# Fixing the order of matrix products, loads and gathers in the expert part of a layer

## The chip, the cores and the metric

The kernel runs on one core of one Trainium2 chip. The metric is the device time of one launch in microseconds (us). Before the change the median of three runs is 2456.3 us (2455.87 to 2461.42). The core has five engines that take instructions in order from queues of their own: TensorE (PE) for matrix products, VectorE (DVE), ScalarE (ACT), GpSimd (POOL) and SyncE (SP). SP, ACT and POOL also issue DMA transfers. An instruction that waits for something holds up all that stands behind it on its engine.

## The reference, cut to what matters

The layer mixes 256 tokens of width 2048 by an mLSTM and by differential attention, and then passes each token through experts that it picks itself (PEER). Only this last part is touched by the change:

```
q = h @ w_pq                                    # 8 heads, two halves each
s = einsum(q, sub_keys)                         # 128 scores per half
s1, i1 = top_k(s[half 0], 16);  s2, i2 = top_k(s[half 1], 16)
top_s, pos = top_k(s1[:, None] + s2[None, :], 16)     # 16 of 256 pairs
idx = (i1 * 128 + i2) at pos                    # 16 experts of 16384 per head
g   = softmax(top_s)
act = gelu(h . expert_u[idx])                   # expert_u: 16384 x 2048
out = sum over the picked experts of g * act * expert_v[idx]
```

A token has 8 x 16 = 128 picked experts. An expert has a first index i1 and a second i2, each of 128 values.

## The kernel before, in words

Everything up to the queries runs until 1167 us of the profiled execution and is untouched, instruction by instruction. Two stages follow.

**The stage of the up-projections, 1167 to 2059 us.** The kernel doesn't gather rows of `expert_u`; it reads all of it, 128 MB, as 256 loads of 512 KB on SP's queue (line 94), two for each value of i1. A load lands in a `raw` tile, ACT copies it to a rounded `hi` (line 108), DVE, and for every fourth POOL, makes the remainder `lo` (line 111), and PE multiplies all 256 tokens with `hi` and `lo` in pairs of products (lines 1191 and 1192): 16 pairs for each i1. The result goes through GELU and is written to a table in memory, `ag_dram`, that has a row for each (i1, i2).

Beside this loop runs a second program, a Python generator (`plan`, line 1376) of which `pump(rate)` does so many steps after each half of an i1. It has the picks of the tokens (`retrieve`, twice, for 128 tokens each), the gate map (`gate_map`, twice) and the lists (`lists`). The gate map turns picks into a dense table: for four tokens at a time `one_hots` (line 1202) makes two one-hot tiles, `o1` by ACT (five activations) and `o2` by POOL (four comparisons, line 1209), PE multiplies them (line 1243), ACT copies the product to `gates`, and SP writes `gates` beside the activations into `ag_dram` in 32 pieces of 512 KB (line 1221), on the same queue as the loads of `expert_u`. The lists sort the experts that are used at all into 99 blocks of 128, by which groups of 32 tokens use them; their one-hots come from the same helper, with PE's products in line 1355. A count, `n_over`, tells whether any expert found no place.

**The stage of the down-projections, 2059 to about 2435 us.** The blocks are multiplied with rows of `expert_v`. A row block (1 MB, 128 rows of 8 KB) is gathered by POOL into one of eight `vraw` halves (line 1409, source `expert_v`), and its gates and activations by another gather from `ag_dram` into an `ag` tile (same line, 128x512 for a block that serves both token halves, 128x256 else). DVE multiplies gate and activation (`w`, line 1446, or line 1443 for the small ones), ACT and DVE split the product into two parts (`l`, lines 1430 and 1431), ACT and DVE split the rows as before, and PE adds up 24 products (a block for both token halves, called B here), 12 (a block for one half, S) or 16 slower ones for a group of four blocks that serve 32 tokens each (G, line 1511, its rows not split). The list ITEMS has 65 entries; from the seventh on it runs G B S B B G B S B B ..., and from the 36th G B B S B G .... A `vraw` half is free again when PE has used both halves of its tile; eight halves hold about one round from G to G.

**What sets the order.** The program is recorded in the order in which Python runs it, and a scheduler then moves instructions within each engine by its own estimate of times. An instruction that is given to `tc.keep_in_program_order` keeps its place among the others so marked on its engine. `next_item(n)` (line 1456) records what the item n of the list needs: first the row gathers of later items, as far as buffers are free, then the gate gathers up to item n + 1; before the change the scheduler moved both as it saw fit.

Of the kernel before, what the change touches and what calls it, by code (L numbers as in the profile page):

```python
# [19 lines left out]
F32 = mybir.dt.float32  # L20
# [10 lines left out]
P = 128  # L31
# [42 lines left out]
def build(tc, a, dump=None):  # L74
    nc = tc.nc
    mm = nc.tensor.matmul
    dump = dump or {}

# [7 lines left out]
    def col(shape, name, src=None, dt=F32):  # L86
# [3 lines left out]
        return t  # L90

    def load(src, pool, bufs, queue=nc.sync):
# [8 lines left out]
    def stage(src, ring=None):  # L101
# [10 lines left out]
        return h, l  # L112

    by_four = [False]

# [996 lines left out]
    def retrieve(t):  # L1112
        def scores(t, i):
            ps = psG.tile([P, 4, P], F32, name="g", tag="g")
            for ii in range(4):
                mm(ps[:, ii, :], lhsT=qT[:, i + ii, t * P:(t + 1) * P], rhs=skT[:, i + ii, :], start=True, stop=True)
# [41 lines left out]
        for s in range(2):  # L1158
            oh = tk.tile([P, HEADS, 16, 16], F32, name="oh", tag="oh", bufs=1)
            for h in range(HEADS):  # L1160
                nc.vector.tensor_tensor(oh[:, h], b3(posf[:, s, h, :], 16),
                                        iota[:, 0:16].unsqueeze(1).to_broadcast([P, 16, 16]), op=OP.is_equal)
                nc.gpsimd.tensor_tensor(oh[:, h], oh[:, h], ti4[:, h, s, :].unsqueeze(1).to_broadcast([P, 16, 16]),
                                        op=OP.mult)
                if h % 2:
                    yield
            r = tk.tile([P, HEADS, 16], F32, name="ix", tag=f"ix{s}", bufs=1)
            nc.vector.reduce_sum(r, oh, axis=AX.X)
            ii.append(r)
            yield  # L1170
        ps = psG.tile([P, 4, P], F32, name="g", tag="g")
        for i, src in enumerate((ii[0], ii[1], e)):
            nc.tensor.transpose(ps[:, i, :], src.rearrange("p h i -> p (h i)"), ident)
            nc.vector.tensor_copy(slots[i][:, t * P:(t + 1) * P], ps[:, i, :])
# [6 lines left out]
    def u_pair(i1, rate):  # L1181
        pss = []
        for e in range(2):
            ps = psS.tile([P, 2, T], F32, name="s", tag="s")
            flat = ps.rearrange("p s t -> p (s t)")
            for hf_ in range(2):
                hl = take()
                for kk in range(8):
                    k = hf_ * 8 + kk
                    w = slice(kk * P, (kk + 1) * P)  # L1190
                    mm(flat, lhsT=hl[0][:, w], rhs=h2hl[k], start=k == 0, stop=False, skip_group_check=True)  # L1191
                    mm(ps[:, 1], lhsT=hl[1][:, w], rhs=h2[0][k], start=False, stop=k == 15, skip_group_check=True)  # L1192
                pump(rate)
            pss.append(ps)
        return pss
# [6 lines left out]
    def one_hots(rows, cols, factor, n=4, width=P):  # L1202
        o1 = gm.tile([P, 4, P], F32, name="o1", tag="o1", bufs=2)
        for i in range(n):
            nc.scalar.activation(o1[:, i], iota, AF.Abs, bias=rows[:, i:i + 1], scale=-1.0)
        nc.scalar.activation(o1[:, 0:n], o1[:, 0:n], AF.Relu, bias=ones[:, 0:1], scale=-1.0)
        o2 = gm.tile([P, 4, P], F32, name="o2", tag="o2", bufs=2)
# [19 lines left out]
    def gate_map(t):  # L1227
# [3 lines left out]

        nxt = hots(0)
        yield
        for hf_ in range(2):
            gates = [gm.tile([P, P // 2, HT], F32, name="gates", tag="gates", bufs=4) for _ in range(2)]
            for q in range(0, HT, 4):
                o1, o2 = nxt
                at = hf_ * HT + q + 4
                if at < P:
                    nxt = hots(at)  # L1240
                ps = psG.tile([P, 4, P], F32, name="g", tag="g")
                for i in range(4):
                    mm(ps[:, i, :], lhsT=o1[:, i], rhs=o2[:, i], start=True, stop=True)  # L1243
                for j in range(2):
# [14 lines left out]
    def lists():  # L1259
# [34 lines left out]
        def fill(kind, first):  # L1294
# [3 lines left out]
                        for _ in range(2))  # L1298
            mm(pre, lhsT=tri, rhs=flat, start=True, stop=True)
            mm(tot, lhsT=ones, rhs=flat, start=True, stop=True)  # L1300
            nc.vector.memset(put[:, 0:n], 0.0)
# [44 lines left out]

        nxt = hots(0)
        ps = psG.tile([P, 4, P], F32, name="g", tag="g")
        yield
        for i in range(0, N_LIST, 4):  # L1350
            o1, o2 = nxt
            if i + 4 < N_LIST:
                nxt = hots(i + 4)
            for j in range(min(4, N_LIST - i)):
                mm(ps[:, 0, 0:N_BLOCKS], lhsT=o1[:, j], rhs=o2[:, j, 0:N_BLOCKS], start=i + j == 0,  # L1355
                   stop=i + j == N_LIST - 1)
            yield
        mm(ps[:, 1, 0:N_LIST], lhsT=ones, rhs=over, start=True, stop=True)
        nc.vector.reduce_sum(t0[:, 0:1], ps[:, 1, 0:N_LIST], axis=AX.X)
# [168 lines left out]

    rest = nc.values_load(n_over[0:1, 0:1], min_val=0, max_val=N_EXPERTS)
    with tc.If(rest > 0):  # L1530
# [32 lines left out]
    def residual(t, c):  # L1563
        w = slice(c * 512, (c + 1) * 512)
        x = x1[t][:, w]
        y = fn.tile([P, 512], F32, name="yf", tag="yf", bufs=2)
        nc.vector.tensor_tensor(y, out_acc[t][c], g2[:, w], op=OP.mult)
# [107 lines left out]
```

## Time and profile before

| | us |
|---|---|
| median of three runs | 2456.3 |
| the profiled execution | 2458.69 |
| its span on the core | 2456.8 |
| PE busy in it | 2335.6 (95%) |
| stage of the up-projections | 1167 to 2059 |
| stage of the down-projections, with the tail | 2059 to 2456.8 |

The span runs from the first to the last instruction of the core; 1.9 us of the execution lie outside it. Busy times of engines overlap; what a stage costs is read from the engine that works without gaps in it, and from what this engine waited for where it did not. PE's busy time includes products that run at half the clock, so the granted clock of a stretch belongs to it.

### The profile page before, as it was taken

Reading aid. Unit: us, or ns where it says so; the run is one execution under the profiler, and the core shown is the slowest. Engines: PE = TensorE matmul, PEld = TensorE weight load, DVE = VectorE, ACT = ScalarE, POOL = GpSimd, SP = SyncE. Lnnn points to the kernel's source line nnn. Section 1 sums busy time; section 2 is a strip of 40 time slices with the busy share of each in tenths; the row PEclk is TensorE's granted clock in tenths of the full one; section 3 lists DMA queues with packets and bytes.
Section 4 is the critical chain, followed back from the end, with each engine's and each line's share of the span. In section 5 each row is a group of like instructions: output and inputs, shape, how many; then the busy total and the mean of one; then the engine's idle time right before and its main releaser. Section 6 shows DMA issues by size and latency. Waiting matters only on the chain. (4 is left out here: it accounts for less than half of the span.)

```text
span 2456.8 us, 38269 instructions
## 1 busy us (share of the span) xinstructions
PE 2335.6 (95%) x14434; PEld 1982.1 (81%) x14434; DVE 1488.2 (61%) x2613; ACT 1138.1 (46%) x1913; POOL 1071.6 (44%) x1101
## 2 busy tenths in 40 slices
PE   6999999999999999999989989999899997999996
PEld 3679989998898999789878878788688886666664
DVE  3457864668766778564986865555744343454445
ACT  3231321245558444444445765677355652333333
POOL 2132201245642100000365895689254775566652
PEclk9999999999999999999999989998999998999998
DMA  9959845875545888665546566766766566899984
GB/s 383 339 209 326 315 166 200 281 213 167 144 155 141 270 279 285 220 194 185 184 152 204 176 186 202 213 196 187 204 199 195 181 236 228 326 361 347 358 319 171
DMA packets 235899, 571.04 MB, mean 232 GB/s; under 512 B 85138, under 2 KB 118723, under 8 KB 221248
## 3 DMA queue, kind: packets, MB, share of 16 engines
q1 hardware_dynamic: 153744, 338.29, 42.7%
q0 software_dynamic: 47120, 212.72, 24.4%
q10 hardware_dynamic: 34848, 17.57, 2.5%
q8 instruction: 113, 1.85, 0.3%
q14 instruction: 74, 0.61, 0.1%
HBM read 524.33 MB, written 38.93 MB: 229 GB/s over the span
## 5 line engine op out<-in xcount | busy, mean ns | idle before, releaser
L108 ACT CAST hi<-raw 128x1024 fp32r<-128x1024 f32 x528 | 552.4, 1048 | 800.9 <-PE acc L265 239.9
L111 DVE TENSOR_TENSOR lo<-raw,hi 128x1024 fp32r<-128x1024 f32 x465 | 599.3, 1291 | 455.3 <-ACT hi L108 455.0
L1191 PE MATMUL s<-h,hi 128*128 128x512 f32 x2048 | 741.5, 402 | 0.5 <-ACT hi L108 0.5
L1192 PE MATMUL s<-h,lo 128*128 128x256 f32 x2048 | 587.7, 288 | 16.2 <-DVE lo L111 8.3
L1191 PEld LDWEIGHTS s<-h,hi 128*128 128x128 f32 x2048 | 390.9, 191 | 85.1 <-ACT hi L108 1.6
L265 PE MATMUL acc<-hL,hi 128*128 128x256 f32 x2048 | 420.4, 285 | 0.0
L1192 PEld LDWEIGHTS s<-h,lo 128*128 128x128 f32 x2048 | 393.4, 192 | 21.2 <-DVE lo L111 11.0
L265 PEld LDWEIGHTS acc<-hL,hi 128*128 128x128 f32 x2048 | 339.3, 192 | 4.2 <-issue 3.9
L265 PE MATMUL acc<-hL,lo 128*128 128x256 f32 x1024 | 291.0, 285 | 2.4 <-DVE lo L111 2.4
L1209 POOL TENSOR_SCALAR o<-iota,i1T,gT 128x128 f32<-128x128 f32 x256 | 256.5, 1013 | 38.7 <-PE g L1243 29.5
L111 POOL TENSOR_TENSOR lo<-raw,hi 128x1024 fp32r<-128x1024 f32 x63 | 152.6, 2422 | 194.3 <-ACT hi L108 188.4
L1497 PE MATMUL v<-hi,l 128*128 128x512 f32 x704 | 202.2, 403 | 15.5 <-ACT hi L1422 11.1
L94 POOL DMA_DIRECT2D raw<-w_mod x128 | 67.9, 531 | 302.0 <-DVE raw L498 280.9
L265 PEld LDWEIGHTS acc<-hL,lo 128*128 128x128 f32 x1024 | 196.2, 192 | 4.1 <-DVE lo L111 3.3
L1497 PEld LDWEIGHTS v<-hi,l 128*128 128x128 f32 x704 | 132.5, 191 | 62.8 <-issue 20.0
L1422 ACT CAST hi<-vraw 128x1024 fp32r<-128x1024 f32 x106 | 108.5, 1046 | 146.9 <-PE v L1497 107.2
L498 DVE SCALAR_TENSOR_TENSOR raw<-raw,cr 128x1024 f32<-128x1024 f32 x128 | 154.2, 1218 | 34.6 <-DMA raw<-w_mod 19.6
L1424 DVE TENSOR_TENSOR lo<-vraw,hi 128x1024 fp32r<-128x1024 f32 x106 | 128.4, 1232 | 71.7 <-ACT hi L1422 63.4
L1409 POOL DMA_INDIRECT vraw<-expert_v,idxV x99 | 114.3, 1154 | 83.2 <-PE v L1511 36.0
L1409 POOL DMA_INDIRECT ag<-ag_dram,idxG x99 | 106.0, 1071 | 77.8 <-DVE w L1446 42.8
L265 PE MATMUL acc<-hC,hi 128*128 128x256 f32 x512 | 134.0, 283 | 0.0
L1209 POOL TENSOR_SCALAR o<-iota,hl,number 128x99 f32<-128x99 f32 x126 | 114.9, 923 | 22.1 <-PE g L1355 22.1
(406 smaller groups left out, 3947.5 us busy)
## 6 DMA issues: line engine op xcount, KB each, us to landing
raw<-expert_u SPq DMA_DIRECT2D x256, 512.0 KB, 3.7
raw<-w_in SPq DMA_DIRECT2D x176, 512.0 KB, 4.8
raw<-w_mod POOLq DMA_DIRECT2D x128, 512.0 KB
raw<-w_mod SPq DMA_DIRECT2D x64, 512.0 KB, 7.2
raw<-w_out SPq DMA_DIRECT2D x32, 512.0 KB, 3.4
raw<-w_pq SPq DMA_DIRECT2D x32, 512.0 KB, 3.4
ag_dram<-gates SPq DMA_DIRECT2D x32, 512.0 KB, 6.5
ag_dram<-act ACTq DMA_DIRECT2D x126, 128.0 KB, 4.1
```

Of the source, the lines that this page charges most:

```text
L94: queue.dma_start(r, src)
L108: nc.scalar.copy(h, r)
L111: (nc.vector if shared[0] else nc.gpsimd).tensor_tensor(l, r, h.bitcast(F32), op=OP.subtract)
L265: mm(acc[c][:, g * T:(g + 1) * T], lhsT=hl[sb][:, k2 * 512 + c * P:k2 * 512 + (c + 1) * P], rhs=rhs(sa, g, k), start=first and k2 == 0 and ...
L498: product = nc.vector.scalar_tensor_tensor(r, r, 1.0, cr, op0=OP.mult, op1=OP.mult, accum_out=part[:, h, i:i + 1])
L1191: mm(flat, lhsT=hl[0][:, w], rhs=h2hl[k], start=k == 0, stop=False, skip_group_check=True)
L1192: mm(ps[:, 1], lhsT=hl[1][:, w], rhs=h2[0][k], start=False, stop=k == 15, skip_group_check=True)
L1209: nc.gpsimd.tensor_scalar(o2[:, i, 0:width], iota[:, 0:width], cols[:, i:i + 1], factor[:, i:i + 1], op0=OP.is_equal, op1=OP.mult)
L1409: nc.gpsimd.indirect_dma_start(out=out, out_offset=None, in_=src, in_offset=bass.IndirectOffsetOnAxis(ap=idx[:, b:b + 1], axis=0))
L1422: nc.scalar.copy(h, raw)
L1424: nc.vector.tensor_tensor(l, raw, h.bitcast(F32), op=OP.subtract)
L1497: mm(out_acc[t][hf_ * 2 + c], lhsT=ins[sa], rhs=hl[sb][:, c * 512:(c + 1) * 512], start=first and i == 0, stop=last and i == 2, skip_group ...
```

## The change: what it does

- Products of PE keep their program order (helpers `mp_` and `turn`): the scores and transposes of `retrieve`, the pairs of the up-projections, the products of the gate map and of the lists.
- On SP the loads of `expert_u` and the gate writes keep program order among each other.
- On POOL all gathers keep program order. `next_item(n)` for n > 0 records the gate gathers up to item n + 1 ahead of the row gathers.
- One-hots are made two steps ahead (a list `ready`), with three buffers each instead of two; of the `o2` comparisons every other one goes to DVE.
- `retrieve` sums its index tables in two halves of four heads; a few more `yield`s; the rate of the second program is 1.05 steps for each half instead of 0.9.
- The read of `n_over` by all engines is put behind the newest instruction of each engine at its place in the program, behind the first five items.
- The last sums take a buffer of another pool.

```diff
     def load(src, pool, bufs, queue=nc.sync):
-        queue.dma_start(r, src)
+        d = queue.dma_start(r, src)
+        if by_four[0]:
+            tc.keep_in_program_order(d)
...
     def u_pair(i1, rate):
-                    mm(flat, lhsT=hl[0][:, w], rhs=h2hl[k], start=k == 0, stop=False, skip_group_check=True)
-                    mm(ps[:, 1], lhsT=hl[1][:, w], rhs=h2[0][k], start=False, stop=k == 15, skip_group_check=True)
+                    mp_(flat, lhsT=hl[0][:, w], rhs=h2hl[k], start=k == 0, stop=False, skip_group_check=True)
+                    mp_(ps[:, 1], lhsT=hl[1][:, w], rhs=h2[0][k], start=False, stop=k == 15, skip_group_check=True)
...
     def one_hots(rows, cols, factor, n=4, width=P):
-        o1 = gm.tile([P, 4, P], F32, name="o1", tag="o1", bufs=2)
+        o1 = gm.tile([P, 4, P], F32, name="o1", tag="o1", bufs=3)
...
-            nc.gpsimd.tensor_scalar(o2[:, i, 0:width], iota[:, 0:width], cols[:, i:i + 1], factor[:, i:i + 1],
+            (nc.gpsimd if i % 2 else nc.vector).tensor_scalar(o2[:, i, 0:width], iota[:, 0:width], cols[:, i:i + 1], factor[:, i:i + 1],
...
             if i % 16 == 0:
-                nc.sync.dma_start(rows[:, i:i + 16, w], g[:, j:j + 16, :])
+                tc.keep_in_program_order(nc.sync.dma_start(rows[:, i:i + 16, w], g[:, j:j + 16, :]))
...
-        nxt = hots(0)
+        ready = [hots(0)]
+        yield
+        ready.append(hots(4))
...
-                o1, o2 = nxt
+                o1, o2 = ready.pop(0)
                 at = hf_ * HT + q + 4
-                if at < P:
-                    nxt = hots(at)
+                if at + 4 < P:
+                    ready.append(hots(at + 4))
...
     def gather(out, src, idx, b):
-        nc.gpsimd.indirect_dma_start(out=out, out_offset=None, in_=src,
-                                     in_offset=bass.IndirectOffsetOnAxis(ap=idx[:, b:b + 1], axis=0))
+        tc.keep_in_program_order(nc.gpsimd.indirect_dma_start(
+            out=out, out_offset=None, in_=src, in_offset=bass.IndirectOffsetOnAxis(ap=idx[:, b:b + 1], axis=0)))
...
+    def fetch_gates(n):
+        while staged[1] < min(len(ITEMS), n):
+            gates_in.append([stage_gates(*b) for b in ITEMS[staged[1]]])
+            staged[1] += 1
+
     def next_item(n):
+        if n:
+            fetch_gates(n + 2)
         while staged[0] < len(ITEMS) and (FIRST_OF[staged[0] + 1] - 1) // 2 * 2 - 7 < FIRST_OF[n]:
             rows_in.append([stage_rows(*b) for b in ITEMS[staged[0]]])
             staged[0] += 1
-        while staged[1] < min(len(ITEMS), n + 2):
-            gates_in.append([stage_gates(*b) for b in ITEMS[staged[1]]])
-            staged[1] += 1
+        fetch_gates(n + 2)
...
-        pss = u_pair(i1, 0.9)
+        pss = u_pair(i1, 1.05)
...
+    with ExitStack() as places:
+        newest = {i.engine: i for i in nc.cur_bb.bb.instructions}
+        for i in newest.values():
+            places.enter_context(tc.issue_after(i))
+        rest = nc.values_load(n_over[0:1, 0:1], min_val=0, max_val=N_EXPERTS)
```

SP's queue in the middle of the gate map before, where `raw<-expert_u` are loads and `ag_dram<-gates` are gate writes:

```order
L94 DMA raw<-expert_u 128x1024 x35
L1221 DMA ag_dram<-gates 128x16x64 x3
L94 DMA raw<-expert_u 128x1024
L1221 DMA ag_dram<-gates 128x16x64 x5
L94 DMA raw<-expert_u 128x1024 x24
```

The same queue in the changed kernel, about the same place:

```order
L104 DMA raw<-expert_u 128x1024 x4
L1235 DMA ag_dram<-gates 128x16x64
L104 DMA raw<-expert_u 128x1024 x11
L1235 DMA ag_dram<-gates 128x16x64
L104 DMA raw<-expert_u 128x1024 x2
```

Gate writes that stood in runs of three and five between loads now stand one at a time, with one to eleven loads between any two.

POOL's queue in the down-projection stage before, one round, where `vraw<-expert_v` are row gathers (the four of a group G stand together) and `ag<-ag_dram` gate gathers:

```order
L1409 DMA ag<-ag_dram,idxG 128x512 x2
L1409 DMA vraw<-expert_v,idxV 128x2048 x4
L1409 DMA ag<-ag_dram,idxG 128x256 x4
L1409 DMA vraw<-expert_v,idxV 128x2048 x2
L1409 DMA ag<-ag_dram,idxG 128x512
L1409 DMA ag<-ag_dram,idxG 128x256
L1409 DMA vraw<-expert_v,idxV 128x2048 x2
```

The same place in the changed kernel, with buffer numbers. `vraw_20993` and `vraw_20996` are the rows of the group G11 (item 11); `ag_21043` and `ag_21071` hold the gates of B9 and B10; `vraw_21073` are rows of B12 and S13; the four 128x256 gathers are gates of G11, `ag_21172` those of B12:

```order
L1429 DMA vraw_20993<-expert_v,idxV_10954 128x2048 x2
L1429 DMA vraw_20996<-expert_v,idxV_10954 128x2048 x2
L1429 DMA ag_21043<-ag_dram_83,idxG_10955 128x512
L1429 DMA ag_21071<-ag_dram_83,idxG_10955 128x512
L1429 DMA vraw_21073<-expert_v,idxV_10954 128x2048 x2
L1429 DMA ag_21120<-ag_dram_83,idxG_10955 128x256
L1429 DMA ag_21122<-ag_dram_83,idxG_10955 128x256
L1429 DMA ag_21124<-ag_dram_83,idxG_10955 128x256
L1429 DMA ag_21126<-ag_dram_83,idxG_10955 128x256
L1429 DMA ag_21172<-ag_dram_83,idxG_10955 128x512
```

The gate gathers of the two blocks B stood ahead of the four row gathers of a group and now stand behind them. In the list, B9 is the third item behind the group G6, whose buffers the rows of G11 take over.

## Rows read from the trace of the kernel before

**Rows 1.** The page of the kernel before: its span, the busy time of each engine, its share of the span and its instructions.

```profile
span 2456.8 us, 38269 instructions
...
PE 2335.6 (95%) x14434; PEld 1982.1 (81%) x14434; DVE 1488.2 (61%) x2613; ACT 1138.1 (46%) x1913; POOL 1071.6 (44%) x1101
```

**Rows 2.** Busy time by stretches of the span; columns are the stretch, its length, the busy time of each engine with its count of instructions, the granted TensorE clock, the DMA engines' busy share and GB/s. The first row lies in the stage of the up-projections, the other three in that of the down-projections.

```profile
1400.00:1460.00 60.00, 48.78 (x270) 42.35 (x269) 39.51 (x57) 39.67 (x89) 60.00 (x61) 0.89 0.70 185
...
2059.00:2100.00 41.00, 26.91 (x92) 19.44 (x91) 15.56 (x40) 11.60 (x20) 26.57 (x27) 0.75 0.49 156
2100.00:2200.00 100.00, 98.39 (x424) 63.23 (x425) 45.03 (x85) 35.37 (x52) 57.97 (x53) 1.00 0.94 373
...
2300.00:2400.00 100.00, 100.00 (x415) 61.19 (x414) 45.56 (x86) 34.72 (x53) 52.68 (x47) 1.00 0.86 334
```

**Rows 3.** Stretches of the up-projection stage, of line 1191 on PE alone: the stretch, its length, busy time and number of its products (16 belong to one value of i1), then clock, DMA share and GB/s of the stretch.

```profile
1167.00:1260.00 93.00, 80.61 (x225) 0.96 0.53 166
...
1400.00:1460.00 60.00, 36.32 (x93) 0.89 0.70 185
1460.00:1550.00 90.00, 83.32 (x238) 1.00 0.63 199
1550.00:1590.00 40.00, 24.19 (x65) 0.91 0.87 220
...
1760.00:1960.00 200.00, 183.16 (x519) 1.00 0.62 191
...
2010.00:2059.00 49.00, 43.41 (x117) 0.93 0.83 318
```

**Rows 4.** The same of line 1243 on PE alone, the products of the gate map.

```profile
1400.00:1460.00 60.00, 14.87 (x84) 0.89 0.70 185
1460.00:1550.00 90.00, 9.22 (x64) 1.00 0.63 199
1550.00:1590.00 40.00, 12.88 (x56) 0.91 0.87 220
```

**Rows 5.** The same of line 1355 on PE alone, the products of the lists.

```profile
1760.00:1960.00 200.00, 23.50 (x168) 1.00 0.62 191
```

**Rows 6.** What PE waited for in the up-projection stage (1150 to 2020 us): engine, line and tile that waited, engine and line that released it, total us, times, the longest.

```profile
PE g L1243 <- POOL o L1209: 10.3, 22, 1.3
PE g L1299 <- DVE k L1323: 9.8, 1, 9.8
PE s L1192 <- DVE lo L111: 7.6, 4, 4.5
...
PE g L1243 <- ACT o L1206: 4.2, 2, 3.9
```

**Rows 7.** SP's queue in order of time, merged: start, us taken, engine, line, operation, tiles, count.

```profile
1556.86 11.00 SPq L1221 DMA_DIRECT2D ag_dram<-gates  x5
1567.96 21.03 SPq L94 DMA_DIRECT2D raw<-expert_u  x8
```

**Rows 8.** The group of POOL's comparisons from 1167 to 2059 us: line, engine, operation, tiles, shapes, count, then busy us, mean ns of one, idle time before them and what ended it.

```profile
L1209 POOL TENSOR_SCALAR o<-iota,i1T,gT 128x128 f32<-128x128 f32 x256 | 256.5, 1013 | 38.7 <-PE g L1243 29.5 <-DVE gT L1174 9.2
```

**Rows 9.** Line 1270 on DVE, an instruction of the same operation as that of rows 8: count, shortest, median and longest duration in ns, first and last start, shape.

```profile
L1270 DVE TENSOR_SCALAR number<-iota,t x1: 286/286/286, 1560.4 to 1560.4; 128x126 f32<-128x126 f32 x1
```

**Rows 10.** What PE waited for from 2059 us to the end, columns as in rows 6.

```profile
PE v L1497 <- ACT hi L1422: 11.1, 2, 7.7
PE v L1497 <- issue: 4.4, 4, 2.2
PE v L1497 <- DVE lo L1424: 1.6, 2, 1.0
```

**Rows 11.** POOL's queue in order of time over one round of the down-projection stage: start, us taken, engine, line, operation, tiles, count, and in brackets the idle time before it and what ended it.

```profile
2201.15 0.94 POOL L1409 DMA_INDIRECT vraw<-expert_v,idxV  x1 [1.93 <-PE v L1511]
...
2205.95 1.97 POOL L1409 DMA_INDIRECT vraw<-expert_v,idxV  x1 [0.30 <-issue]
...
2229.08 0.94 POOL L1409 DMA_INDIRECT vraw<-expert_v,idxV  x1 [1.93 <-PE v L1511]
```

**Rows 12.** PE in order of time in the same round, from the end of its group of four on, columns as in the rows before.

```profile
2203.40 2.13 PE L1497 MATMUL v<-hi,l 128*128 128x512 f32 x8
...
2211.41 2.48 PE L1497 MATMUL v<-hi,l 128*128 128x512 f32 x10
2213.73 0.62 PE L1497 MATMUL v<-lo,l 128*128 128x512 f32 x2
```

**Rows 13.** The DMA view from 2100 to 2400 us: GB/s in 40 slices of 7.5 us.

```profile
GB/s 245 374 419 421 416 424 387 376 341 354 362 330 394 304 428 303 409 280 404 327 386 319 341 355 331 380 416 223 380 397 413 270 407 332 347 249 421 417 85 372
```

**Rows 14.** Groups of instructions from 2100 to 2400 us: line, engine, operation, tiles, shapes, count, then busy us, mean ns of one, idle time before them and what ended it.

```profile
L1430 ACT CAST l<-w 128x128 fp32r<-128x128 f32 x72 | 21.3, 297 | 80.2 <-PE v L1497 57.6 <-issue 17.0 <-DVE lo L1424 3.2
L1431 DVE TENSOR_TENSOR l<-w,l 128x128 fp32r<-128x128 f32 x70 | 19.2, 288 | 61.8 <-PE v L1497 60.9 <-issue 0.6 <-ACT l L1430 0.3
L1446 DVE TENSOR_TENSOR w<-ag 128x128 f32<-128x128 f32 x70 | 18.4, 287 | 0.9
```

**Rows 15.** Three short stretches: one in which PE stood for some us, the one behind it, and one behind PE's longest wait in the down-projection stage; columns as in rows 2.

```profile
2016.00:2020.00 4.00, 1.45 (x9) 0.99 (x7) 1.31 (x2) 0.63 (x1) 3.65 (x3) 1.00 1.02 425
2020.00:2027.00 7.00, 5.90 (x18) 5.07 (x19) 1.23 (x1) 2.02 (x2) 1.04 (x1) 0.51 1.01 418
...
2079.00:2096.00 17.00, 10.78 (x25) 7.59 (x26) 5.91 (x11) 3.94 (x7) 8.36 (x8) 0.52 0.49 176
```

More of the change, by code (lines that the diff above doesn't have):

```diff
@@ L76, in build, with mp_, turn @@
     mm = nc.tensor.matmul
+    def mp_(*args, **kw):
+        tc.keep_in_program_order(mm(*args, **kw))
+    def turn(*args):
+        tc.keep_in_program_order(nc.tensor.transpose(*args))
     dump = dump or {}
@@ L112, in stage @@
         return h, l
-    by_four = [False]
     def pieces():
@@ L1115, in scores @@
             for ii in range(4):
-                mm(ps[:, ii, :], lhsT=qT[:, i + ii, t * P:(t + 1) * P], rhs=skT[:, i + ii, :], start=True, stop=True)
+                mp_(ps[:, ii, :], lhsT=qT[:, i + ii, t * P:(t + 1) * P], rhs=skT[:, i + ii, :], start=True, stop=True)
             sc = tk.tile([P, 4, P], F32, name="sc", tag="sc", bufs=2)
@@ L1158, in retrieve @@
         for s in range(2):
-            oh = tk.tile([P, HEADS, 16, 16], F32, name="oh", tag="oh", bufs=1)
+            r = tk.tile([P, HEADS, 16], F32, name="ix", tag=f"ix{s}", bufs=1)
             for h in range(HEADS):
-                nc.vector.tensor_tensor(oh[:, h], b3(posf[:, s, h, :], 16),
+                if h % 4 == 0:
+                    four = tk.tile([P, 4, 16, 16], F32, name="oh", tag="oh", bufs=1)
+                oh = four[:, h % 4]
+                nc.vector.tensor_tensor(oh, b3(posf[:, s, h, :], 16),
                                         iota[:, 0:16].unsqueeze(1).to_broadcast([P, 16, 16]), op=OP.is_equal)
-                nc.gpsimd.tensor_tensor(oh[:, h], oh[:, h], ti4[:, h, s, :].unsqueeze(1).to_broadcast([P, 16, 16]),
+                nc.gpsimd.tensor_tensor(oh, oh, ti4[:, h, s, :].unsqueeze(1).to_broadcast([P, 16, 16]),
                                         op=OP.mult)
+                if h % 4 == 3:
+                    yield
+                    nc.vector.reduce_sum(r[:, h - 3:h + 1], four, axis=AX.X)
                 if h % 2:
                     yield
-            r = tk.tile([P, HEADS, 16], F32, name="ix", tag=f"ix{s}", bufs=1)
-            nc.vector.reduce_sum(r, oh, axis=AX.X)
             ii.append(r)
-            yield
+        yield
         ps = psG.tile([P, 4, P], F32, name="g", tag="g")
         for i, src in enumerate((ii[0], ii[1], e)):
-            nc.tensor.transpose(ps[:, i, :], src.rearrange("p h i -> p (h i)"), ident)
+            turn(ps[:, i, :], src.rearrange("p h i -> p (h i)"), ident)
             nc.vector.tensor_copy(slots[i][:, t * P:(t + 1) * P], ps[:, i, :])
@@ L1206, in one_hots @@
         nc.scalar.activation(o1[:, 0:n], o1[:, 0:n], AF.Relu, bias=ones[:, 0:1], scale=-1.0)
-        o2 = gm.tile([P, 4, P], F32, name="o2", tag="o2", bufs=2)
+        o2 = gm.tile([P, 4, P], F32, name="o2", tag="o2", bufs=3)
         for i in range(n):
-            nc.gpsimd.tensor_scalar(o2[:, i, 0:width], iota[:, 0:width], cols[:, i:i + 1], factor[:, i:i + 1],
+            (nc.gpsimd if i % 2 else nc.vector).tensor_scalar(o2[:, i, 0:width], iota[:, 0:width], cols[:, i:i + 1], factor[:, i:i + 1],
                                     op0=OP.is_equal, op1=OP.mult)
@@ L1298, in fill @@
                         for _ in range(2))
-            mm(pre, lhsT=tri, rhs=flat, start=True, stop=True)
-            mm(tot, lhsT=ones, rhs=flat, start=True, stop=True)
+            yield
+            yield
+            mp_(pre, lhsT=tri, rhs=flat, start=True, stop=True)
+            mp_(tot, lhsT=ones, rhs=flat, start=True, stop=True)
             nc.vector.memset(put[:, 0:n], 0.0)
@@ L1345, in hots @@
             return one_hots(hl[:, 1, w], hl[:, 0, w], number[:, w], w.stop - i, N_BLOCKS)
-        nxt = hots(0)
+        ready = [hots(0)]
+        yield
+        ready.append(hots(4))
         ps = psG.tile([P, 4, P], F32, name="g", tag="g")
@@ L1350, in lists @@
         for i in range(0, N_LIST, 4):
-            o1, o2 = nxt
-            if i + 4 < N_LIST:
-                nxt = hots(i + 4)
+            o1, o2 = ready.pop(0)
+            if i + 8 < N_LIST:
+                ready.append(hots(i + 8))
             for j in range(min(4, N_LIST - i)):
-                mm(ps[:, 0, 0:N_BLOCKS], lhsT=o1[:, j], rhs=o2[:, j, 0:N_BLOCKS], start=i + j == 0,
+                mp_(ps[:, 0, 0:N_BLOCKS], lhsT=o1[:, j], rhs=o2[:, j, 0:N_BLOCKS], start=i + j == 0,
                    stop=i + j == N_LIST - 1)
             yield
-        mm(ps[:, 1, 0:N_LIST], lhsT=ones, rhs=over, start=True, stop=True)
+        mp_(ps[:, 1, 0:N_LIST], lhsT=ones, rhs=over, start=True, stop=True)
         nc.vector.reduce_sum(t0[:, 0:1], ps[:, 1, 0:N_LIST], axis=AX.X)
@@ L1565, in residual @@
         x = x1[t][:, w]
-        y = fn.tile([P, 512], F32, name="yf", tag="yf", bufs=2)
+        y = gm.tile([P, 4, P], F32, name="yf", tag="o1", bufs=3).rearrange("p a b -> p (a b)")
         nc.vector.tensor_tensor(y, out_acc[t][c], g2[:, w], op=OP.mult)
```

5 lines of the change are left out of this document (3 added, 2 removed).

## The prediction

> **What bounds the kernel now.** I read the page first: PE is busy 95% of the span [rows 1], so time is lost only where PE stands, or where it runs at half the clock. Then the stretches of each stage, then PE's waits, then the queues of SP and POOL at the places found.
>
> In the up-projections I take what one pair of products costs from two stretches without waits. From 1460 to 1550 us 238 pairs and 64 records of gate products fill 90 us; from 1760 to 1960 us 519 pairs and 168 records of list products fill 200 us [rows 3 to 5]. Taking a gate record and a list record as equal, that gives 0.343 us for a pair and 0.131 us for a record. The stage has 128 x 16 = 2048 pairs, 512 gate and 252 list records: 702 + 67 + 33 = 802 us, against 892 (1167 to 2059). Of the 90 us some 10 are other products (scores, transposes, counts), so about 80 us are lost. By stretch, in the same way: 1167 to 1260 loses 93 - 225 x 0.343 = 16 (perhaps 12 of them waits, the rest score products); 1400 to 1460 loses 60 - 31.9 - 11.0 = 17; 1550 to 1590 loses 40 - 22.3 - 7.3 = 10; 2010 to 2059 loses 9. One wait of 9.8 us on DVE [rows 6] costs 15 with the half clock behind it. The other 15 to 20 us are spread.
>
> The causes: from 1400 to 1460 POOL is busy for all 60 us [rows 2] and PE waits for its comparisons (10.3 us in 22 waits [rows 6]). At 1556.86 SP issues five gate writes in 11.00 us, and the next load goes out only at 1567.96 [rows 7].
>
> In the down-projections PE has waits only before 2100 us: 17.1 us in all [rows 10], and 2079 to 2096 at a clock of 0.52 [rows 15], where 10.8 us of PE's work could have taken half, another 5.5. From 2100 to 2400 PE is busy without a gap worth naming [rows 2], a round from G to G takes 2229.08 - 2201.15 = 27.93 us [rows 11], and the DMA engines run at 0.86 to 0.94 [rows 2]. So there PE is the bound, and the gathers are close behind.
>
> **The change part by part.**
>
> *Comparisons shared with DVE.* POOL's 256 comparisons of the gate map take 1.013 us each [rows 8]. Half of them leave it, 128 x 1.013 = 130 us, besides 63 of the lists'. On DVE the nearest row is one TENSOR_SCALAR of 0.286 us [rows 9]: 191 x 0.286 = 55 us more, and DVE is busy 39.5 of the 60 us where POOL is full [rows 2]. This and the regular steps remove POOL as the bound from 1400 to 1460: I take 13 of 17 us.
>
> *SP's queue.* With gate writes one at a time between loads the 11 us hole goes; a write costs about 11.00 / 5 = 2.2 us of SP's queue, and a load is due every 2.8 us (half of 16 x 0.343). I take 9 of 10 us at 1550.
>
> *Two yields ahead of the counts.* They let DVE finish before PE reaches line 1299: 13 of 15 us. *The earlier lists and the read of the count behind the fifth item* take work out of the last loads: 6 of 9. *Half sums in retrieve*: 5 of 12, since DVE's sorting itself stays. The spread rest, of which some belongs to the same two causes, gives 10 of 20. What is added: PE's pinned pairs can now stand behind a gate product whose one-hots are late, where the scheduler could have slipped a pair in; the nearest row is 4.2 us in two waits on ACT [rows 6]; I take 6, at most 15. Sum: 13 + 9 + 13 + 6 + 5 + 10 - 6 = 50 us gained, with ends of 25 and 75. The up-projections end at 2058.9 - 50 = 2009.
>
> *Gathers pinned on POOL.* This is the place that decides. In before a round on POOL is gate gathers of two B, then the four row gathers of the next G, which wait for PE to finish the group before it: the first at 2201.15, the last issued at 2205.95 and 1.97 us long [rows 11]. The gates are several items ahead. After, gates are asked for one item ahead, and the order puts the gates of B9 behind the rows of G11. Those rows wait for G6's last products, and between G6 and B9 PE has only B7 and S8.
>
> I count from the end E of a group. PE's products go every 2.32 / 10 = 0.232 us [rows 12], so B7 and S8 last (24 + 12) x 0.232 = 8.4 us; in the next rounds 3 products of the B slip ahead of the group's end, and 7.7 are left. The first row gather goes at about E - 1 (before it was 2203.40 - 2201.15 = 2.2 us ahead of the end [rows 11, 12]; the new order of G's products frees the first tile two of sixteen products before its end). Four rows are 4.19 MB. At 353 GB/s, the middle of the 373 and 334 of rows 2, that is 11.9 us, at the 424 of the best slices 9.9 [rows 13]. With 1 us for the first issue the rows land at E + 10 to E + 12. The small gates were issued behind them and land with them or 0.5 us later. Then come `w` 0.287, the copy 0.297 and the remainder 0.288 us [rows 14]; 0.9 in sum. B9 can start at E + 11.2 to E + 13.4 and is due at E + 7.7 to 8.4: a stall of 2.8 to 5.7 us. I take 4.7, nearer to the mean rate than to the best slices, in six rounds: 28 us. From item 35 on two B and one S lie between (60 products, 13.9 us), but five or six rows are staged, a pair of them only free after the first B (5.6 us behind E): 5.6 + 11 is E + 16.6, with the weights 17.5, a stall of 3.6, in five rounds: 18. Where PE has stood for some 3 us of four (busy 1.45 of 2016 to 2020), the next 7 us run at a granted clock of 0.51, that is 1.2 instead of 2.4 GHz [rows 15], and cost 3.5 us. I put 3 us to each of the eleven rounds: 33. Together 79 us, with ends of 0 (all gates in time) and 11 x (6.5 + 5) = 125.
>
> The Trainium skill, DMA: Bandwidth & Descriptors, section "Where 436 GB/s comes from", has two limits: about 358 GB/s for a core's share of the memory, and 435 GB/s for the ports. The mean of rows 2 agrees with the first, single slices of rows 13 lie above it. By an estimate at 435 the four rows take 9.6 us, and each stall would be 2.3 us shorter than with the mean rate, 25 us in eleven rounds.
>
> *The start of the down-projections.* The first row gathers stand behind POOL's last `lo`, and the first gates behind four rows; by the same count they land about 5 us after the last pair, 8 with the clock. The gates of the first G stand behind the `n_over` branch and a 1 MB load: 8 more. The early losses of before (17.1 + 5.5 = 22.6) go.
>
> *Nothing:* the last sums' buffer, at the end of a tail that stays.
>
> **The sum.** From 2058.9 to the end before takes 397.9 us; without its 22.6 us of early loss 375.3. After: 2009 + 375.3 + 8 + 8 + 79 = 2479 of span, 2481 of execution with the 1.9 us outside. The profiled execution (2458.69) is 2.4 above the median of 2456.3, so 2478 on the scale of the median: 22 us slower.
>
> **The rivals.**
>
> *The gates come in time (faster).* The gate gather is small, POOL needs only 7 us for four row issues, and PE has 7.7 to 13.9 us of other work; if rows land at the best slices' rate, the stall is 2 us or less, and the clock stays. Then 11 x 2 = 22 in place of 79, and with 5 in place of each 8: 2009 + 375.3 + 10 + 22 + 1.9 - 2.4 = 2416; with no stall at all 2394. For it: slices above 400 GB/s [rows 13]. Against it: the mean.
>
> *Gain and loss cancel (same).* Stalls of 4 us of which half drop the clock: 11 x (4 + 1.5) = 60, or a gain of 70 in the up-projections: 2449 to 2464.
>
> *Later work is caught behind the gates as well (slower still).* DVE's new order puts the products `w` of a later B ahead of the remainder of the B in work. If those gates come after that remainder is needed, PE stops a second time in a round: 2 us in eleven rounds, and 2500. It decides from the point at which the rows of the next two items land later than 22 us behind E. The pinned pairs at their upper price (15 for 6) would add 9.
>
> **How the numbers follow.** Forecast 0.46, caught work 0.10, cancel 0.14, gates in time 0.30. A measurement here tells 0.3%, about 7 us, from nothing; so slower 0.56, same 0.14, faster 0.30. The forecast's own range is 2464 to 2505. The range for 8 in 10 reaches up to 2520 (the caught work) and down to 2408, into the case of gates in time.
>
> **What would show it.** Right: from 2060 us on PE waits for `w` or `l` once a round, 3 to 6 us, behind POOL's row gathers that wait for line 1536, rounds of 33 to 36 us instead of 27.93, and granted clocks below 1.00. The up-projections end near 2009, with no run of gate writes on SP and POOL below full from 1400 to 1460. Wrong: rounds of about 28 us (then the gates land earlier than I count), or an end of the up-projections past 2035.

## The result, and the profile after

The changed kernel takes 2481.8 us (median of five runs, 2477.6 to 2487.4) where the kernel before takes 2455.9 (median of five): a ratio of 1.0109, with a 95% interval of 1.0085 to 1.0133. It is slower by 1.1%. The forecast was 2478.

The page of the changed kernel, to be held against [rows 1]:

```profile
span 2480.6 us, 38079 instructions
...
PE 2304.3 (93%) x14434; PEld 1970.7 (79%) x14434; DVE 1545.8 (62%) x2808; ACT 1139.0 (46%) x1913; POOL 897.0 (36%) x910
```

PE is busy 31 us less and the span 24 us longer, so PE stands some 55 us more. Where, the stretches say (columns as in [rows 2]):

```profile
1400.00:1460.00 60.00, 53.70 (x308) 46.96 (x308) 46.41 (x66) 37.03 (x73) 39.06 (x33) 0.94 0.71 198
...
2100.00:2200.00 100.00, 77.25 (x340) 50.75 (x339) 41.06 (x78) 29.00 (x44) 51.84 (x48) 0.90 0.77 295
...
2300.00:2400.00 100.00, 77.79 (x346) 54.18 (x345) 39.82 (x78) 29.52 (x45) 52.16 (x48) 0.86 0.74 294
```

From 1400 to 1460 POOL is busy 39 of 60 us instead of all, and PE 53.7 instead of 48.8. From 2100 to 2400, where PE had no gap before, it now stands for more than a fifth of the time, the granted clock is 0.90 and 0.86 in these rows, and the DMA engines, at 0.94 and 0.86 before, are at 0.77 and 0.74 and have time to spare: nothing is short there, something is late.

The up-projections themselves: the last of their products before and after (line, operation, count, durations in ns, first and last start, shape).

```profile
L1192 PE MATMUL s<-h,lo x2048: 274/280/582, 1167.3 to 2058.8; 128*128 128x256 f32 x187
```

```profile
L80 PE MATMUL s<-h,lo x2048: 274/280/579, 1169.3 to 2021.2; 128*128 128x256 f32 x187
```

The stage took 891.5 us and takes 851.9: a gain of 39.6. From its end to the end of the span were 398.0 us and are 459.4: a loss of 61.4. The difference of 21.8, with the 2.0 us by which the stage starts later, is the 24 us of the spans.

PE's waits in the down-projections (columns as in [rows 6]), which answer to [rows 10]:

```profile
PE v L1522 <- ACT l L1450: 82.4, 12, 8.3
PE v L1536 <- DVE w L1463: 6.1, 1, 6.1
```

One of the twelve is at the change of stages (6.7 us), one of 3.4 in the first items; the other ten, 72 us, come one in each round. One round, first POOL (as [rows 11]), then PE (as [rows 12]):

```profile
2144.57 1.03 POOL L1429 DMA_INDIRECT vraw<-expert_v,idxV  x1 [3.96 <-PE v L1536]
...
2148.38 1.88 POOL L1429 DMA_INDIRECT vraw<-expert_v,idxV  x1 [0.31 <-issue]
2150.57 0.95 POOL L1429 DMA_INDIRECT ag<-ag_dram,idxG  x1 [0.30 <-issue]
...
2178.46 1.07 POOL L1429 DMA_INDIRECT vraw<-expert_v,idxV  x1 [4.97 <-PE v L1536]
```

```profile
2142.38 1.92 PE L1536 MATMUL v<-vraw,w 128*32 128x512 f32 x16
...
2152.00 0.63 PE L1522 MATMUL v<-hi,l 128*128 128x512 f32 x2
2160.20 1.22 PE L1522 MATMUL v<-hi,l 128*128 128x512 f32 x2 [7.57 <-ACT l L1450]
...
2163.63 0.63 PE L1522 MATMUL v<-hi,l 128*128 128x512 f32 x2
```

And DVE, which makes the weights from the gates:

```profile
2159.53 0.49 DVE L1466 TENSOR_TENSOR w<-ag 128x128 f32<-128x128 f32 x2 [4.56 <-DMA ag<-ag_dram,idxG]
```

The group ends at 2144.3. POOL had waited for it (3.96 us, released by PE) and sends four row gathers from 2144.57 on; the gates' gather stands behind them, goes out at 2150.57, and its data are there at 2159.5, when DVE, which had waited for the DMA, multiplies them. ACT and DVE make `l`, and PE goes on at 2160.20, 7.6 us after its last product. Rounds last 2178.46 - 2144.57 = 33.9 us instead of 27.93.

### The profile page after: what moved, and what is told of

Same layout as the page of the kernel before. It is cut to its first block, busy times and chain, and to the rows that moved or that the text cites. A ratio compares the mean times of both kernels' runs of the same rounds, so it can differ in the third digit from the quotient of the medians.

```text
span 2480.6 us, 38079 instructions
## 1 busy us (share of the span) xinstructions
PE 2304.3 (93%) x14434; PEld 1970.7 (79%) x14434; DVE 1545.8 (62%) x2808; ACT 1139.0 (46%) x1913; POOL 897.0 (36%) x910
## 5 line engine op out<-in xcount | busy, mean ns | idle before, releaser
L123 DVE TENSOR_TENSOR lo<-raw,hi 128x1024 fp32r<-128x1024 f32 x465 | 591.6, 1275 | 330.4 <-ACT hi L120 329.5
L80 PE MATMUL s<-h,lo 128*128 128x256 f32 x2048 | 578.2, 282 | 18.8 <-DVE lo L123 11.6
L1522 PE MATMUL v<-hi,l 128*128 128x512 f32 x704 | 217.3, 422 | 84.1 <-ACT l L1450 82.4
L1522 PEld LDWEIGHTS v<-hi,l 128*128 128x128 f32 x704 | 138.5, 201 | 139.2 <-ACT l L1450 88.7
L1223 POOL TENSOR_SCALAR o<-iota,i1T,gT 128x128 f32<-128x128 f32 x128 | 141.2, 1110 | 90.4 <-PE g L80 48.1
L1429 POOL DMA_INDIRECT vraw<-expert_v,idxV x99 | 104.5, 1056 | 168.2 <-PE v L1536 90.5
L1522 PE MATMUL v<-lo,l 128*128 128x512 f32 x352 | 122.4, 429 | 2.8 <-DVE lo L1444 2.8
```

The costliest lines, as they stand in the source:

```text
L80: tc.keep_in_program_order(mm(*args, **kw))
L123: (nc.vector if shared[0] else nc.gpsimd).tensor_tensor(l, r, h.bitcast(F32), op=OP.subtract)
L1223: (nc.gpsimd if i % 2 else nc.vector).tensor_scalar(o2[:, i, 0:width], iota[:, 0:width], cols[:, i:i + 1], factor[:, i:i + 1], op0=OP.is_e ...
L1429: tc.keep_in_program_order(nc.gpsimd.indirect_dma_start(out=out, out_offset=None, in_=src, in_offset=bass.IndirectOffsetOnAxis(ap=idx[:, b ...
L1522: mm(out_acc[t][hf_ * 2 + c], lhsT=ins[sa], rhs=hl[sb][:, c * 512:(c + 1) * 512], start=first and i == 0, stop=last and i == 2, skip_group ...
```

## The experiments

Each kernel is timed beside the kernel before on the same chip; ratios are to that. The four kernels of experiment 7 ran once each; there the stage of the up-projections is read from the trace.

**1. Are the gathers alone to blame?** The kernel before, with only POOL's gathers fixed and in the changed kernel's order:

```diff
-        nc.gpsimd.indirect_dma_start(out=out, ...
+        tc.keep_in_program_order(nc.gpsimd.indirect_dma_start(out=out, ...
...
+        if n:
+            fetch_gates(n + 2)
```

> The kernel before with only the gathers fixed on POOL, in the order of the changed kernel. Theory: the up-projections end near 2059 as before, and the down-projections take what they take in the changed kernel (459 us to the end instead of 398), so 2510 to 2520 us. If the stalls came from another part of the change, it stays within 2440 to 2475.

Measured: 2519.5 us, 1.0281 (1.0264 to 1.0299), and PE's waits of the changed kernel are there again:

```profile
PE v L1502 <- ACT l L1430: 81.5, 12, 8.0
PE v L1516 <- DVE w L1443: 5.8, 1, 5.8
```

So this part alone costs 69 us, and nothing of the other parts is needed for it. The time lies at the upper end of the range expected.

**2. The changed kernel without it.** Gathers left to the scheduler, all else as changed:

```diff
-        tc.keep_in_program_order(nc.gpsimd.indirect_dma_start(
-            out=out, ...
+        nc.gpsimd.indirect_dma_start(
+            out=out, ...
```

> The changed kernel with the gathers left to the scheduler, as before. Theory: only the down-projections change; the up-projections end near 2021 as in the changed kernel, and from there it runs as the kernel before did (398 us to the end), about 2415 to 2425 us. If the gain of the up-projections hung on the fixed gathers, their end would move back towards 2059, and the time towards 2456.

Measured: 2413.3 us, 0.9847 (0.9831 to 0.9863), a little below the range expected. The gain of the up-projections doesn't hang on the gathers: their last product starts at 2027. Against the 2481.8 us of the changed kernel, fixing the gathers costs 68 us here too.

**3. Is it the order, or that the order is fixed?** One number changed, gates two items further ahead:

```diff
         if n:
-            fetch_gates(n + 2)
+            fetch_gates(n + 4)
```

> The changed kernel with one number changed: gates are recorded up to item n + 3 instead of n + 1 ahead of the rows, still in fixed order on POOL. Theory (gates queue behind the four row gathers of a group): the stalls of 6.6 to 8.3 us in each round go, with the half clock behind them, at the same bytes; a round falls from 34.1 to 24 to 28 us, and the time to about 2370 to 2400 us. Rival (the transfers themselves are the limit, or fixing POOL's order as such costs): rounds stay above 32 us, time above 2460.

Measured: 2413.5 us, 0.9845 (0.9827 to 0.9862). From 2100 us on no round has a stall of PE worth naming; one wait of 6.8 us at the change of stages is left. The bytes are the same and the order is still fixed, so the stalls were the place of the gates in the queue: the theory holds, the rival falls. The time, though, is 13 us above the expected range. The reason stands in PE's groups of four, of this kernel and of the kernel before:

```profile
2143.20 8.86 PE L1536 MATMUL v<-vraw,w 128*32 128x512 f32 x32
2171.78 8.86 PE L1536 MATMUL v<-vraw,w 128*32 128x512 f32 x32
```

```profile
2220.33 1.90 PE L1511 MATMUL v<-vraw,w 128*32 128x512 f32 x4
2225.14 6.26 PE L1511 MATMUL v<-vraw,w 128*32 128x512 f32 x28
```

In the changed kernel the 16 records (8 products) of 2142.38 took 1.92 us; here all 32 take 8.86, and before they took 8.2. What differs is the order of the sixteen products. Each of the four blocks of a group has weights of 32 columns and writes its own strip of 32 rows of the result. Where the four products of a strip stand side by side, as in this kernel, the sixteen take 0.55 us each on average; where neighbours belong to different strips, 0.23. That the order makes this difference is shown by experiment 4.

**4. The group's order by itself.** The kernel before, with only these products kept in program order, in which neighbours always differ in strip:

```diff
     def v_groups(t, parts):
         for c in range(4):
             for j, (raw, ins) in enumerate(parts):
-                mm(out_acc[t][c][32 * j:32 * j + 32, :], ...)
+                tc.keep_in_program_order(mm(out_acc[t][c][32 * j:32 * j + 32, :], ...))
```

> The kernel before with only the sixteen products of a group of four kept in program order, in which neighbours belong to different 32-column strips. Theory (neighbours of one strip run one after the other, of different strips together): a group takes about 3.7 instead of 8.2 us, a round falls from 27.93 to 23.5 to 25 us, the time by 35 to 48 us, to 2410 to 2420. Rival (the groups are quicker in the changed kernel because PE had waited and everything was there): groups stay at 8 us, time 2450 to 2460.

Measured: 2413.1 us, 0.9842 (0.9825 to 0.9859), 37 us less, and the groups:

```profile
2140.73 3.64 PE L1511 MATMUL v<-vraw,w 128*32 128x512 f32 x32
2164.09 3.64 PE L1511 MATMUL v<-vraw,w 128*32 128x512 f32 x32
```

A round is 2164.09 - 2140.73 = 23.4 us. It is the order, with no wait of PE needed to make the groups short. The loads of weights ahead of the products (engine PEld) come every 0.43 us, mostly one or two at a time in experiment 3 and four at a time here:

```profile
2144.09 0.11 PEld L1536 LDWEIGHTS v<-vraw,w 128*32 128x32 f32 x1 [0.32 <-issue]
2147.12 0.14 PEld L1536 LDWEIGHTS v<-vraw,w 128*32 128x32 f32 x2 [0.29 <-issue]
```

```profile
2141.61 0.13 PEld L1511 LDWEIGHTS v<-vraw,w 128*32 128x32 f32 x4 [0.30 <-issue]
```

The change doesn't touch this loop; by moving the gathers it led the scheduler to another order there, and so won back a part of what it lost. The kernel of experiment 1, in which only the gathers differ from the kernel before, has short groups too, of some 4.9 us in three pieces:

```profile
2132.86 1.93 PE L1516 MATMUL v<-vraw,w 128*32 128x512 f32 x14
2135.84 1.04 PE L1516 MATMUL v<-vraw,w 128*32 128x512 f32 x2
2138.87 1.92 PE L1516 MATMUL v<-vraw,w 128*32 128x512 f32 x16
```

**5. Both together.** Gates three items ahead and the groups in program order; and, with the gathers free, the groups in program order:

> e1_gates_ahead with the products of a group kept in program order (neighbours in different strips). There a group took 8.86 us with four neighbours in one strip. Theory: 3.64 us each, twelve times 5.2 us less: 2350 to 2365 us; less gain, down to 2375 us, if the DMA engines become the bound of a round (about 9.9 MB at 420 GB/s are 23.5 us). Rival: order of a group's products doesn't matter, 2413.

> e2_gathers_free with the products of a group kept in program order. Theory: as e3_group_order did for the kernel before, 37 to 46 us less than e2_gathers_free: 2367 to 2377 us. It tells by comparison with e6_ahead_and_order whether a fixed order of gathers with gates three items ahead is as good as the scheduler's.

Measured: 2376.5 us, 0.9686 (0.9668 to 0.9704), and 2380.0 us, 0.970 (0.9674 to 0.9726). The first is 37 us below the same kernel without the group's order, 1.5 us above the upper end expected, the second 33 us below its own and 3 us above the range. Why not 2350 to 2365, the first shows in part, by two stretches (columns as in [rows 2]), two of its groups and one of its waits:

```profile
2100.00:2200.00 100.00, 99.36 (x489) 70.86 (x490) 58.67 (x113) 44.17 (x67) 72.42 (x69) 1.00 1.01 413
2200.00:2300.00 100.00, 93.39 (x451) 64.50 (x450) 50.27 (x103) 37.02 (x59) 70.23 (x64) 1.00 0.98 392
```

```profile
2143.79 3.64 PE L80 MATMUL v<-vraw,w 128*32 128x512 f32 x32
2167.22 3.64 PE L80 MATMUL v<-vraw,w 128*32 128x512 f32 x32
...
2212.47 3.62 PE L80 MATMUL v<-vraw,w 128*32 128x512 f32 x26 [1.45 <-DMA vraw<-expert_v,idxV]
```

In the first stretch PE is busy 99% of the time, and the DMA engines are full as well, at 413 GB/s. A round takes 2167.22 - 2143.79 = 23.4 us, which is the 28.6 of experiment 3 less the 5.2 by which a group is shorter, so PE has its whole gain there. In the second stretch PE stands for 6.6 us, 1.9 of them directly for rows, with the DMA engines at 0.98; that they are what holds PE there in all is likely, but not shown. Besides, the up-projections of this execution end 10 us later than in that of experiment 3 (2028.6 against 2018.1), which is within what kernels with the same stage differ by (experiment 7) and has nothing to do with the groups. The stalls stay away here with short groups too, so it was not the longer groups of experiment 3 that hid them. Against these two versions the changed kernel is 4% slower, with the same work.

**6. One item further ahead instead of two.** As the first of the two, with `fetch_gates(n + 3)`:

> The changed kernel with gates recorded up to item n + 2 (one more than there, one less than in e1_gates_ahead), and the products of a group kept in program order. Theory: the gates that stand behind the rows of a group now belong to the item that is due 13.9 us behind the end of the group before, and land some 14.4 us behind it: stalls of 1 to 3 us, at which the clock mostly stays. Rounds of 24 to 26 us, time 2360 to 2385 us. Rival (any fixed order with gates behind rows costs the whole wait again): 2420 or more.

Measured: 2400.0 us, 0.9778 (0.9759 to 0.9798). Between the two, but above the expected range. PE's waits from 2100 to 2400 us:

```profile
PE v L80 <- DVE w L1463: 11.5, 10, 3.2
PE v L1522 <- ACT l L1450: 6.2, 4, 2.0
```

The stalls on `l`, of 0.9 to 2.0 us, are as expected; but now PE waits for the gates of the group itself as well (`w` of line 1463), up to 3.2 us at a time, a wait that the expectation left out.

**7. The gain of the up-projections, part by part.** Four kernels, each the changed one without one part: all comparisons on POOL; gate writes on SP left to the scheduler; no yields ahead of the counts; pairs left to the scheduler.

```diff
-            (nc.gpsimd if i % 2 else nc.vector).tensor_scalar(o2[:, i, 0:width], ...
+            nc.gpsimd.tensor_scalar(o2[:, i, 0:width], ...
```

> The changed kernel with all o2 comparisons on POOL again. If sharing them with DVE is what removed POOL as the bound near 1430 us, the up-projections end 10 to 15 us later than 2021.5 us, and POOL is full there again. If the steady steps and the fixed order did it, the end moves by less than 4 us. The rest of the kernel is the same.

```diff
-                tc.keep_in_program_order(nc.sync.dma_start(rows[:, i:i + 16, w], g[:, j:j + 16, :]))
+                nc.sync.dma_start(rows[:, i:i + 16, w], g[:, j:j + 16, :])
```

> The changed kernel with the gate writes on SP left to the scheduler. The stage of the up-projections (first to last of its products) took 891.7 us before and 852.2 us after. If the runs of gate writes between loads cost what the prediction says (9 us), it rises to 858 to 864 us; if loads are far enough ahead, it stays at 849 to 855 us. Down-projections as in the changed kernel.

```diff
-            yield
-            yield
             mp_(pre, lhsT=tri, rhs=flat, start=True, stop=True)
```

> The changed kernel without the two yields ahead of the counts. Prediction: the wait of PE for DVE of 9.8 us near 1739 us comes back, and with it 13 us: the stage takes 862 to 867 us. Rival: the fixed order and the steady steps already keep DVE ahead, and it stays at 849 to 855 us.

```diff
-                    mp_(flat, lhsT=hl[0][:, w], ...
-                    mp_(ps[:, 1], lhsT=hl[1][:, w], ...
+                    mm(flat, lhsT=hl[0][:, w], ...
+                    mm(ps[:, 1], lhsT=hl[1][:, w], ...
```

> The changed kernel with the pairs of the up-projections left to the scheduler. The prediction puts the cost of fixing them at 6 us: the stage would then take 843 to 849 us. Rival: free pairs move between the gate products by the scheduler's own times and PE waits more often for one-hots: 855 us or more.

Measured, from the first to the last start of the stage's products: 885, 892, 849 and 851 us, against 852 after and 892 before. The times, of one run each, agree: 2515, 2516, 2481 and 2479 us. Kernels whose stage is the same differ by up to 9 us (the two of experiments 1 and 4, which have that of before, took 885 and 897; the six of experiments 2, 3, 5, 6 and 8, which have that of after, 849 to 861), so only the first two tell anything.

Without the sharing 33 us of the 39.6 are gone, and with that scatter perhaps all. But not where the expectation looked: from 1400 to 1460 us POOL is busy for 57 of 60 us, and PE for 56.6, more than in the changed kernel. From 1550 to 1650 us POOL is full, which it is not after the change; first the kernel with all comparisons on POOL, then the changed one:

```profile
1550.00:1590.00 40.00, 34.96 (x213) 31.20 (x212) 21.23 (x29) 31.71 (x75) 40.00 (x40) 0.91 0.71 191
1590.00:1650.00 60.00, 55.73 (x352) 49.59 (x350) 37.15 (x48) 53.87 (x126) 60.00 (x60) 0.97 0.73 196
```

```profile
1550.00:1590.00 40.00, 40.00 (x262) 36.17 (x261) 33.49 (x59) 38.23 (x92) 31.41 (x26) 1.00 0.81 228
1590.00:1650.00 60.00, 59.34 (x385) 53.21 (x384) 45.98 (x82) 53.40 (x129) 42.62 (x34) 1.00 0.83 220
```

What PE waits for there is not the comparisons but the remainders `lo` that POOL makes on the same queue:

```profile
PE s L80 <- POOL lo L123: 34.3, 16, 5.0
```

Without the fixed writes all 40 us are gone. SP sends writes in runs of up to seven (up to six in the kernel before), and PE stands behind the loads; SP's queue and PE's longest row of waits:

```profile
1519.63 12.70 SPq L1235 DMA_DIRECT2D ag_dram<-gates  x5
1532.43 71.30 SPq L104 DMA_DIRECT2D raw<-expert_u  x21
```

```profile
PE s L80 <- ACT hi L120: 36.6, 6, 11.0
```

In the changed kernel each of the two is needed, and neither brings the gain without the other: 33 and 40 do not add up to 39.6. Why is shown only in part. Two limits lie at one place in the kernel before: from 1567 us on PE goes from one comparison of POOL to the next, and the load behind SP's five writes [rows 7] is copied by ACT only at 1575.4.

```profile
1567.70 0.49 PE L1243 MATMUL g<-o,o 128*128 128x128 f32 x2 [0.28 <-POOL o L1209]
...
1575.43 1.03 ACT L108 CAST hi<-raw 128x1024 fp32r<-128x1024 f32 x1
```

But the long waits of these two kernels are not those of the kernel before, where PE waited 4.2 us for POOL's remainders and 0.2 for ACT's copies (1150 to 2020 us). Both kernels keep the one-hots made two steps ahead and the faster rate of the second program, which put more work into the same time; whether these make the loss larger was not tried. The yields and the fixed pairs show nothing beyond the scatter, neither gain nor cost; PE's wait of 9.8 us on DVE is gone without the yields too, and which part removed it was not tried.

**8. The change of stages.** The version of experiment 5 with fewer row gathers ahead of the first gates:

```diff
-        while staged[0] < len(ITEMS) and (FIRST_OF...
+        while staged[0] < (len(ITEMS) if n else 2) and (FIRST_OF...
```

> e6_ahead_and_order, with the row gathers of only the first two items recorded ahead of the first gates (four gathers were issued there at 2008.5 to 2013.6 us, and the last load of the up-projections, the last writes of activations and with them the first gates came only some 15 us later). Theory (4 MB of early rows share the DMA engines with that load and those writes): with half of them the first gates go out some 5 us earlier, PE's waits of 3.7 and 4.5 us at the change of stages shrink and the clock stays up: 5 to 12 us less than e6_ahead_and_order, 2364 to 2372 us. Rival (the gates wait for the last product's activations in any case): the same, 2372 to 2381 us, or later rows cost as much elsewhere.

Measured: 2379.3 us, 0.9705 (0.9682 to 0.9729), no different from 0.9686. POOL still waits for 13.3 us before the first gates (14.9 without this edit), and PE 7.5 us (3.7 and 4.5 without it). So the early rows are not what holds the gates there. What does is open; that it is the writes of the last activations was not tried.

## Why the prediction was right, and where by luck

The direction, the place and the mechanism hold as they were put: gates queued on POOL behind rows that wait for PE, in each round. Experiment 1 shows that this alone makes the kernel slower, experiments 3 and 5 that the place in the queue does it. That the total of 2478 came so near to 2482 is luck: several of its terms were off and cancelled.

- *The up-projections.* 50 us were forecast, 39.6 came (the ends were 25 and 75), so 10 too much. The split was wrong: SP's writes were put at 9 us and are needed for all of it, the sharing was put at 13 and is needed for 33. One row was misread: the 10.3 us of [rows 6] are PE's waits for comparisons in the whole stage, and from 1400 to 1460 us they are 4.0. The step that failed added up the losses of single places, as if each had one cause and its removal gave back just that; experiment 7 shows that the two parts don't add up, and why only in part. The 13 us for the yields and the 6 us taken off for the fixed pairs did not show. The price of a comparison on DVE, 0.286 us from [rows 9], was low as well: 128 of them took 0.422 us each in the mean and 63 took 0.354, together 68 us of DVE's busy time where 55 were forecast.
- *The stall of a round* was put at 4.7 us, at most 5.7, in six rounds and at 3.6 in five later ones. It is 5.6 to 8.3 in the trace, in ten rounds, and no shorter in the later ones. Two pieces of the count failed. The first row was to go 1 us before the group's end; it went 0.3 us behind it, in a group whose last eight products took only 1.9 us. And the rate was counted from the first moment: the engines moved 282 GB/s in the mean from 2144 to 2152 us, and 410 from 2153 on:

```profile
2144.00:2152.00 8.00, 8.00 (x38) 6.32 (x34) 3.59 (x5) 3.06 (x4) 5.91 (x6) 1.00 0.76 282
2153.00:2160.00 7.00, 0.00 (x0) 0.00 (x0) 2.33 (x4) 0.86 (x2) 5.17 (x7) 0.76 1.00 410
2160.00:2164.00 4.00, 3.80 (x10) 3.03 (x11) 1.41 (x7) 0.85 (x4) 1.78 (x2) 0.57 1.00 421
```

- *The half clock* was put at 3 us a round. The granted clock was already at the lower level, 1.2 GHz, for a part of the time in which PE was still waiting (0.76 in the mean of 2153 to 2160), and from 2163.63 on products take their usual time again, so only some eight ran slow: 2163.63 - 2160.20 = 3.4 us where eight at 0.232 take 1.9. The price in this round is 1.6 us.
- *The groups' length* is the term that was put at nothing without a reason: the prediction names the new order of a group's products, for the time at which a tile comes free, and gives it no price. They took 8 us and take about 4.3 in the changed kernel's rounds. A round is then 27.9 + 7.6 + 1.6 - 3.7 = 33.4, measured 33.9; the forecast for it was 27.9 + 4.7 + 3 = 35.6.
- *The start of the stage* (5 us and the clock) was 6.7, the first group's gates (5 and the clock) 6.1. The early losses of before went, as forecast, but for a wait of 3.4. But the first group took 10.7 us where it had taken 4.7, and from the end of the up-projections to the end of the second group it is 89.5 us after 88.8 before: 0.7 more, where 16 less 22.6, or 6.6 less, were forecast. The tail behind the last group, put at nothing, is 4.1 us longer. The ten rounds between the two cost 57 us more than before, where 79 were forecast for eleven.

In sum the up-projections' gain was put 10 us too high and the loss behind them about as much too high (72 us for 61.4: 8 + 8 + 79 less 22.6); within that loss, stalls that were too short in the forecast stand against groups that became shorter. Of the two limits in the Trainium skill (DMA: Bandwidth & Descriptors, section "Where 436 GB/s comes from") the lower, about 358 GB/s, does not bind here: 410 GB/s were moved during the stall and 413 over 100 us in experiment 5, nearer to the upper one. The estimate made with the upper one, stalls 2.3 us shorter, did not come true either: the start of the gathers took what the rate gave.

The rival in which gates come in time fell in every round; that of work caught behind the gates a second time in a round was not seen. The one that no rival named is the change of the groups' order.

## What to carry to other kernels

An order that is fixed in a queue has to be read for what each instruction waits for: a small transfer that is due early must not stand behind large ones that wait for the engine which needs the small one. Before the gain of an edit is read off a wait, look for a second limit at the same place, as POOL and SP at 1567 us here; in this kernel neither of the two edits brought its gain without the other. And compare the order of instructions that the change does not touch: a scheduler may move these too, and what it gives or takes there hides in the total.

## What the runs showed of the hardware that was not expected

Products with 32 columns of weights that write different strips of 32 rows run together, if they stand side by side: sixteen take 3.64 us, 0.23 us each on average, and 8.86 us, or 0.55 each, where the four of one strip are neighbours. The order alone is worth 37 us here (experiment 4). With it, and the gates three items ahead, the DMA engines carry 413 GB/s over 100 us, most of it in gathers of rows of 8 KB, where the stage had run at 334 to 373 GB/s before.
